# A hybrid trunk step on one core: the side-work unit of a DeltaNet inverse step set from 1.368 to 1.207

## The chip, the core and the metric

The kernel runs on one core of one Trainium2 chip. The metric is the device time of one execution in microseconds (us). The rows shown here come from one profiled execution, which the hardware profiler recorded. In them PE is the matrix engine, PEld its weight load, DVE the vector engine, ACT the scalar engine, POOL the general engine, and SP the engine whose queue starts nearly all transfers (SPq).

## What is computed

Two layers of a trunk run on 640 tokens (128 of a prompt, 512 of a sample), with 1024 channels. Each layer has one wide input projection whose columns feed three branches, a mix, and a feed-forward network. Only the first part of a layer matters here:

```
h  = RMSNorm(x) * (1 + scale1) + shift1
ya = (cb * conv(cc * cx)) @ w_pa              # short gated conv, 4 blocks of 128 channels
yb = attention(q, k, v) @ w_pb                # 8 heads, 2 kv heads, 128 cached + 512 sample keys
yc = (norm(deltanet_fwd + deltanet_bwd) * silu(z)) @ w_pc      # 4 heads, 2 directions
mix = (sigmoid(g0)*ya + sigmoid(g1)*yb + sigmoid(g2)*yc) @ w_o
```

DeltaNet needs, for each head, direction and chunk of 128 tokens, the inverse of a unit triangular matrix. The kernel inverts its 32x32 diagonal blocks by elimination, and joins them with small matmuls to 64x64 and 128x128.

## The kernel before

**Layout.** Channels lie on the 128 partitions and tokens along the free axis, in two halves of 320. Float32 products are made of three matmuls in the fp32r type: each operand is split into a high and a low part (`split`, a cast on ACT at L94 and a subtraction on DVE at L95), and `mm3` (L363 to L365) adds high*high, high*low and low*high. `linear` makes one block of 128 output channels: for eight input blocks, two halves and three products that is 48 matmuls; with four input blocks, as for `w_pc`, it is 24. Its weights come in pieces of 256 KB (`wraw`, issued at L359, three buffers), and the split parts have three buffers each (`whi`, `wlo`).

**Main work and side work.** The first part of each layer is traced from two Python generators. `mainc` holds the chains that wait much: two pairs of DeltaNet heads (`delta_pair`, then `dn_out`), then the keys and values, then eight attention heads (`attn_head`, with the next head's `attn_q` traced inside each). `fillc` holds side work for PE: the z blocks, the conv branch (12 blocks), then for eight output blocks a gate (`g0`) and a `w_pa` product, eight gates `g2` and four gates `g1` (each stored to DRAM in `sgd`), and, once all four heads of DeltaNet are done, the eight `w_pc` products of `branch(l, 2, ...)`. Here they are called pc0 to pc7. Each pc block loads a gate (`sgl`, L536) and the running mix (`mixo`, L542) from DRAM, multiplies (L442), adds (L545) and stores the mix (L547).

`run` decides how the two are interleaved. Each `yield` of the main work names a number of units, and side work is traced until it has caught up:

```
for c in main:
    tm += c * rate
    while fill is not None and tf < tm:
        t = next(fill)          # traces one more piece of side work
        if t is None:
            tf = tm
            break
        tf += t
```

A block of side work counts 6.5 units, a `w_pc` or `w_pa` product 3.2. The units of the main work stand in a list of constants: Y_QKV 1.127, Y_NAT 4.215, Y_EL 1.368, Y_INV 1.962, Y_SCAN 2.959, Y_O 2.917, Y_DO 2.558 for DeltaNet, Y_AK 0.438, Y_AKK 2.07, Y_AQ 1.037, Y_AT 0.446 for attention. The units set an order of tracing and nothing else; no instruction carries one. The order in which the instructions of one engine then run follows the traced order closely, but is not bound to it: an instruction that is ready may be put ahead of an earlier one that is not.

**The inverse.** In `delta_pair`, after the decay terms of two heads, the 20 blocks are gathered in `D32` and transposed on DVE into `Tt` (L985). The elimination takes 30 steps (L987 to L993) of a multiply (L990) and an add (L992) on DVE, each followed by `yield Y_EL`. Four transposes on DVE (L1000) give `RA` and `RB`, each followed by `yield Y_EL` too, so a pair has 34 such yields. The joining follows for four cases of head and direction, each with two `yield Y_INV`: the first matmuls are at L1020, fed by the masks that DVE writes at L1011. Then come five scan steps and the outputs.

**Buffers.** Full-width float32 tiles come from three shared sets. The set F has 16 buffers (NF_), and all of these hold one: the gates and mixes of side work (`sg`, `sgl`, `mixo`), the split DeltaNet outputs `rsh0..3` and `rsl0..3` that all eight pc blocks read (from `resplit(yf, "F")`), and the attention outputs `o0..o7`. An attention output is held from its first write until `resplit(o, "C")`, which is traced after `run` has ended. A head's first write of it is two stages behind its scores (NPD = 2). The set E has three buffers, for `D32`, `Tt`, `RA`, `RB`, the modulation weights `wm` and the 512 KB table `rope` (L617).

Of the kernel before, what the change touches and what calls it, by code (L numbers as in the profile page):

```python
# [43 lines left out]
NSQ = (0, 0, 0, 0, 0, 0, 0, 1)  # L44
ENDG = (3, 7)

Y_QKV, Y_NAT, Y_EL, Y_INV, Y_SCAN, Y_O = 1.127, 4.215, 1.368, 1.962, 2.959, 2.917
Y_AT, Y_AQ, Y_AK, Y_AKK, Y_DO = 0.446, 1.037, 0.438, 2.07, 2.558
PB, PF = 8.0, 11.5

# [1362 lines left out]
```

## Time and profile before

| | us |
|---|---|
| median of 3 runs | 2832.45 |
| lowest, highest | 2823.55, 2837.19 |
| the profiled execution | 2826.17 |
| its span, first to last instruction | 2824.4 |

The mean granted clock of PE in the profiled execution was 0.983 of full speed. The profiled execution is 1.77 us longer than its span. The first parts of the two layers lie at about 59 to 779 us and 1480 to 2179 us of the span. A row of the windows view gives, for a stretch, each engine's busy time with the number of its instructions, then the granted clock and the share and rate of the transfers. Starts in rows are us from the start of the span.

### The profile page before, as it was taken

The numbers are of one execution on the slowest core, as the hardware profiler recorded it, in microseconds if no ns is written. First come the engines' busy times: TensorE is split into PE (matmuls) and PEld (weight loads), VectorE is DVE, ScalarE is ACT, GpSimd is POOL, SyncE is SP. The second block draws the span as 40 slices with busy tenths as digits, with TensorE's granted clock in tenths as the row PEclk, the third lists the DMA queues.
The fourth block names the chain that finished last, engine by engine and source line by source line (L and its number), as shares of the span: only waits on it lengthen the run. The fifth ranks groups of instructions, "written<-read, shape, count | busy, mean of one in ns | idle before, by whom it ended". The sixth has DMA issues, their size and how long they took to land.

```text
span 2824.4 us, 49743 instructions
## 1 busy us (share of the span) xinstructions
PE 2732.8 (97%) x19706; PEld 2599.2 (92%) x19706; DVE 1560.5 (55%) x3297; ACT 1260.3 (45%) x2863; POOL 113.6 (4%) x235
## 2 busy tenths in 40 slices
PE   7999999999999999999989999999998999999998
PEld 3899998999799899999979999989998999999997
DVE  4586564477743744324466865745777456442344
ACT  4533553455534533223455345535555354332343
POOL 1000000000001200000020000000000020000002
PEclk9999999999999999999999999999999999999999
DMA  8552355444264444444442323433331333222231
GB/s 243 70 79 58 79 87 111 81 91 113 89 157 139 146 131 143 130 157 143 134 115 64 76 56 86 91 92 77 101 98 62 95 105 96 76 73 75 77 119 65
DMA packets 390970, 288.17 MB, mean 102 GB/s; under 512 B 19051, under 2 KB 354641, under 8 KB 390737
## 3 DMA queue, kind: packets, MB, share of 16 engines
q1 hardware_dynamic: 390736, 285.00, 39.2%
q8 instruction: 154, 2.52, 0.4%
q14 instruction: 80, 0.65, 0.1%
HBM read 251.86 MB, written 33.07 MB: 101 GB/s over the span
## 4 chain that ended last, share of the span: by engine, by line
PE 82%; DMA 6%; DVE 6%; ACT 4%; issue 1%; SPq 0%; POOL 0%; ACTq 0%; DVEq 0%; POOLq 0%
PE l L363 22%; PE l L364 22%; PE l L365 22%; DMA wraw<-in_w_in_dram 2%; PE pm L324 1%; DMA rowb<-gd 1%; PE ptT L772 1%; ACT p L727 1%; DMA xo<-xd 1%; PE po L782 1%; DMA sgl<-sgd 1%; PE po L784 1%; PE scan L1073 1%; PE kk L948 1%; PE po L783 1%
## 5 line engine op out<-in xcount | busy, mean ns | idle before, releaser
L94 ACT CAST whi<-wraw 128x512 fp32r<-128x512 f32 (+1 forms) x540 | 332.2, 615 | 847.8 <-PE l L364 784.4
L95 DVE TENSOR_TENSOR wlo<-wraw,whi 128x512 fp32r<-128x512 f32 (+1 forms) x540 | 369.0, 684 | 560.8 <-ACT whi L94 532.1
L363 PE MATMUL l<-hh,whi 128*128 128x320 f32 x1856 | 588.3, 317 | 11.5 <-ACT padc L863 6.0
L364 PE MATMUL l<-hl,whi 128*128 128x320 f32 x1856 | 584.4, 315 | 0.0
L365 PE MATMUL l<-hh,wlo 128*128 128x320 f32 x1856 | 583.9, 315 | 0.0
L363 PE MATMUL l<-h2h,whi 128*128 128x320 f32 x1248 | 387.4, 310 | 0.0
L364 PE MATMUL l<-h2l,whi 128*128 128x320 f32 x1248 | 385.3, 309 | 0.0
L365 PE MATMUL l<-h2h,wlo 128*128 128x320 f32 x1248 | 385.3, 309 | 0.0
L363 PEld LDWEIGHTS l<-hh,whi 128*128 128x128 f32 x1856 | 352.2, 190 | 15.7 <-ACT padc L863 6.7
L364 PEld LDWEIGHTS l<-hl,whi 128*128 128x128 f32 x1856 | 353.1, 190 | 1.9
L365 PEld LDWEIGHTS l<-hh,wlo 128*128 128x128 f32 x1856 | 352.9, 190 | 1.5
L363 PEld LDWEIGHTS l<-h2h,whi 128*128 128x128 f32 x1248 | 234.6, 188 | 7.0 <-ACT fs L427 3.1
L364 PEld LDWEIGHTS l<-h2l,whi 128*128 128x128 f32 x1248 | 234.6, 188 | 0.0
L365 PEld LDWEIGHTS l<-h2h,wlo 128*128 128x128 f32 x1248 | 234.6, 188 | 0.0
L363 PE MATMUL l<-ah,whi 128*128 128x320 f32 x544 | 168.9, 310 | 0.0
L364 PE MATMUL l<-al,whi 128*128 128x320 f32 x544 | 168.1, 309 | 0.0
L365 PE MATMUL l<-ah,wlo 128*128 128x320 f32 x544 | 168.0, 309 | 0.0
L152 POOL TENSOR_TENSOR acc<-acc,sqt 128x320 f32<-128x320 f32 x88 | 87.1, 989 | 2000.4 <-ACT sqt L148 1998.7
L363 PE MATMUL l<-rsh,whi 128*128 128x320 f32 x384 | 120.0, 315 | 0.0
L364 PE MATMUL l<-rsl,whi 128*128 128x320 f32 x384 | 118.2, 311 | 0.0
L365 PE MATMUL l<-rsh,wlo 128*128 128x320 f32 x384 | 118.2, 309 | 0.0
L363 PEld LDWEIGHTS l<-ah,whi 128*128 128x128 f32 x544 | 102.2, 188 | 2.2 <-ACT pt L447 1.7
(428 smaller groups left out, 5453.3 us busy)
## 6 DMA issues: line engine op xcount, KB each, us to landing
wraw<-in_w_in_dram SPq DMA_DIRECT2D x256, 256.0 KB, 4.3
wm<-in_w_mod_dram SPq DMA_DIRECT2D x80, 512.0 KB, 4.8
wraw<-in_w_gate_dram SPq DMA_DIRECT2D x88, 256.0 KB, 2.9
wraw<-in_w_up_dram SPq DMA_DIRECT2D x88, 256.0 KB, 3.1
wraw<-in_w_down_dram SPq DMA_DIRECT2D x80, 256.0 KB, 2.8
mixo<-mixd SPq DMA_DIRECT2D x32, 320.0 KB, 5.4
wm<-in_w_mod_dram SPq DMA_DIRECT2D x32, 256.0 KB, 4.4
wraw<-in_w_pb_dram SPq DMA_DIRECT2D x32, 256.0 KB, 4.4
```

Of the source, the lines that this page charges most:

```text
L94: A.copy(hi, src)
L95: V.tensor_sub(lo, src, hi.bitcast(F32))
L152: (V if n == 2 else G).tensor_add(accs[0], accs[0], t)
L324: T.matmul(pm[32 * u:32 * u + 2, 0:256], lhsT=sc[:, k, :], rhs=w[:, u * 256:(u + 1) * 256], start=(n == 0), stop=(n == KD - 1))
L363: T.matmul(out, lhsT=wh, rhs=ah, start=first, stop=False)
L364: T.matmul(out, lhsT=wh, rhs=al, start=False, stop=False)
L365: T.matmul(out, lhsT=wl, rhs=ah, start=False, stop=last)
L727: A.activation(p[:, o_:o_ + w], x, AF.Exp, scale=rc, bias=nb[:, 0:1], accum_out=s[:, i:i + 1])
L772: T.transpose(pt[:, i, q * P:(q + 1) * P], sm_[q][:, kt * P:(kt + 1) * P], ident)
L782: T.matmul(po, lhsT=vh, rhs=th, start=(kt == 0), stop=False)
L783: T.matmul(po, lhsT=vl, rhs=th, start=False, stop=False)
L784: T.matmul(po, lhsT=vh, rhs=tl, start=False, stop=(kt == 4))
```

## The change

One constant changes:

```diff
-Y_QKV, Y_NAT, Y_EL, Y_INV, Y_SCAN, Y_O = 1.127, 4.215, 1.368, 1.962, 2.959, 2.917
+Y_QKV, Y_NAT, Y_EL, Y_INV, Y_SCAN, Y_O = 1.127, 4.215, 1.207, 1.962, 2.959, 2.917
```

Thirty steps of 1.368 are 41.04 units, and 34 steps of 1.207 are 41.04 units: the unit goes down as the number of yields beside it had gone up, from 30 to 34. Before the change the 34 yields count 46.51 units. No instruction is added or removed; side work is traced later against the main work.

## Rows read from the trace of the kernel before

**Rows 1.** The page, part 1: busy time of each engine.

```profile
PE 2732.8 (97%) x19706; PEld 2599.2 (92%) x19706; DVE 1560.5 (55%) x3297; ACT 1260.3 (45%) x2863; POOL 113.6 (4%) x235
```

**Rows 2.** Windows of 20 us: two in the first pair's elimination, layer 0.

```profile
160.00:180.00 20.00, 20.00 (x139) 20.00 (x138) 19.51 (x47) 5.56 (x12) 1.66 (x10) 1.00 0.40 87
180.00:200.00 20.00, 20.00 (x139) 20.00 (x138) 19.31 (x48) 4.60 (x8) 0.00 (x0) 1.00 0.38 67
```

**Rows 3.** Windows after the second pair's elimination, both layers.

```profile
440.00:450.00 10.00, 10.00 (x70) 10.00 (x69) 1.38 (x2) 3.40 (x6) 0.00 (x0) 1.00 1.02 124
450.00:470.00 20.00, 16.69 (x168) 14.41 (x167) 6.50 (x14) 6.00 (x13) 0.00 (x0) 0.74 0.41 109
1840.00:1855.00 15.00, 15.00 (x110) 14.77 (x110) 3.32 (x6) 6.69 (x12) 0.00 (x0) 1.00 0.74 148
1855.00:1870.00 15.00, 13.16 (x123) 11.36 (x123) 5.17 (x11) 4.61 (x10) 0.00 (x0) 0.67 0.34 95
```

**Rows 4.** Windows: attention with side work and its last 40 us, both layers.

```profile
690.00:740.00 50.00, 49.96 (x369) 47.03 (x369) 38.06 (x103) 30.30 (x88) 0.00 (x0) 1.00 0.32 95
740.00:780.00 40.00, 34.48 (x232) 27.70 (x232) 28.61 (x78) 24.32 (x71) 0.00 (x0) 0.91 0.24 79
2090.00:2140.00 50.00, 49.80 (x362) 47.91 (x361) 38.38 (x104) 29.43 (x84) 0.00 (x0) 1.00 0.27 81
2140.00:2180.00 40.00, 31.75 (x197) 27.66 (x195) 27.76 (x77) 24.05 (x71) 0.00 (x0) 0.87 0.04 9
```

**Rows 5.** Who PE waited for, 1480 to 2190 us: total, times, longest.

```profile
PE psc L363 <- ACT p L727: 5.1, 2, 4.1
```

**Rows 6.** DVE: the last w_pc block's addition in each layer (L545).

```profile
715.60 0.83 DVE L545 TENSOR_TENSOR sgl<-sgl,mixo 128x640 f32<-128x640 f32 x1
...
2119.11 0.82 DVE L545 TENSOR_TENSOR sgl<-sgl,mixo 128x640 f32<-128x640 f32 x1
```

**Rows 7.** Chain of waits and SP's queue, layer 0, second pair: start, length.

```profile
434.98 6.73 DMA wraw<-in_w_in_dram
...
443.18 11.17 DMA wraw<-in_w_in_dram
...
436.14 0.34 SPq L617 DMA_DIRECT2D rope<-in_rope_dram  x1
```

**Rows 8.** DVE in order of time, layer 0: end of the first pair's elimination.

```profile
169.87 2.06 DVE L985 STREAM_TRANSPOSE Tt<-D 128x1024 f32<-128x1024 f32 x1
...
204.37 0.09 DVE L994 MEMSET Tt<- 128x32 f32 x1
204.42 0.22 DVE L992 TENSOR_TENSOR Tt<-Tt,tmpE 128x58 f32<-128x58 f32 x1
...
209.87 0.50 DVE L1011 TENSOR_TENSOR Xq<-RB,cst 128x320 f32<-128x320 f32 x1
```

**Rows 9.** PE at L1020: first joining matmuls (min/median/max ns, first and last start).

```profile
L1020 PE MATMUL pw<-RB,nt x21: 191/191/212, 214.4 to 232.0; 32*32 32x32 f32 x21
L1020 PE MATMUL pw<-RB,nt x20: 191/191/212, 1619.4 to 1621.0; 32*32 32x32 f32 x20
```

**Rows 10.** DVE: masks that release the joining, layer 1's first pair.

```profile
1615.99 0.46 DVE L1011 TENSOR_TENSOR Xq<-RB,cst 128x320 f32<-128x320 f32 x1
```

**Rows 11.** Tiles o and mixo: splitting an attention output, loading the mix.

```profile
L94 ACT CAST rsh<-o x16: 723/728/734, 776.6 to 2183.2; 128x640 fp32r<-128x640 f32 x16
L95 DVE TENSOR_TENSOR rsl<-o,rsh x16: 814/818/826, 777.5 to 2184.3; 128x640 fp32r<-128x640 f32 x16
...
DMA to landing us min/median/max: 3.5/5.4/7.2
```

**Rows 12.** Window of 10 us inside layer 0's last 40 us of attention.

```profile
750.00:760.00 10.00, 9.24 (x46) 7.75 (x46) 6.18 (x20) 5.03 (x16) 0.00 (x0) 0.66 0.32 124
```

## The prediction

> **What bounds the kernel now.** I read the page's busy times first. PE is busy for 97% of the span [rows 1], so only time in which PE stands still, or runs at less than full clock, can be won, and time is lost only where PE is newly made to wait. Then I read windows through the first part of a layer, since the constant orders nothing else. In the elimination PE does 139 matmuls in each 20 us and DVE is busy for 19.3 to 19.5 of them [rows 2]: both are full. 20 us / 139 is 0.144 us for a matmul, so a side block of 48 matmuls is 6.9 us of PE and a pc block of 24 is 3.45 us. These two prices carry most of what follows.
>
> PE is not full in two places. One is after the second pair's elimination: in 450 to 470 us of layer 0 it stands still for 20 - 16.69 = 3.3 us, and the granted clock of the stretch is 0.74; in layer 1 it is 15 - 13.16 = 1.8 us at 0.67 [rows 3]. The reader should see a gap and then the lower of the clock's two levels (1.2 in place of 2.4 GHz) behind it. The other is the end of attention, 740 to 780 us and 2140 to 2180 us: 5.5 us and 8.25 us still, clock 0.91 and 0.87 [rows 4]. There the waits are those of softmax (in layer 1 the prompt's scores wait once for 4.1 us for the exponentials on ACT [rows 5]), and no side work is at hand: the last pc block is added at 715.6 us and at 2119.1 us [rows 6], long before attention ends.
>
> **What the change does to the order.** It follows from the yields by addition. A pair's 34 yields go from 46.51 to 41.04 units. The main work of a layer is, before, 123.4 units for the first pair, 126.8 for the second (three `linear` yields more) and 43.4 for keys, values and heads: 293.6. The side work is 16 blocks at 6.5 (z and conv), eight times 9.7, 12 gates at 6.5 and eight pc at 3.2: 285.2. So before, the side work runs out 8.4 units early: pc7 is traced at unit 282.3, in the first stages of head 5. After, the main work is 282.6 units, and pc7 is traced at 282.2, behind head 7's last scores; pc5 comes in head 6's first stage and pc6 in its second. Ahead of the first joining matmul there stood 84.5 units of side work in the first pair and 214.1 in the second; now it is 78.0 and 201.1. That is one block fewer, and then two fewer. Nothing else moves: no instruction is added, and the transfers of a side block go with it on SP's queue, past those of the main work (two weight pieces, a gate store; for pc one weight piece, `sgl`, `mixo` and a store).
>
> **Part 1, the end of attention.** With side work at hand PE does 369 matmuls in 50 us in layer 0, and 362 in layer 1 [rows 4]. At that rate the 232 and 197 of the last 40 us need 31.4 and 27.2 us, so 8.6 and 12.8 us are lost there, waits and low clock together. The three pc blocks that arrive hold 3 x 3.45 = 10.35 us of PE for each layer, which no longer stands elsewhere. From above the gain is 8.6 + 10.35 = 19.0 us (each layer the smaller of what is lost and what arrives). From below it is nothing: softmax's chain of DVE, ACT and PE might be lengthened by as much as is filled. I take pc5 and pc6 as filling, and pc7, traced behind the last scores, as not: 2 x 3.45 = 6.9 us for each layer, 13.8 us in all, because the heads just before, with this same ratio of side work, leave PE still for 0.04 and 0.2 us in 50 [rows 4].
>
> How much is to be had depends on the row that one trusts. The Trainium skill (Perfetto Trace Analysis, Identifying the Most-Contended Engine) says that matmul occupancy judges TensorE badly, since pipelined matmuls blur it, and that LDWEIGHTS occupancy judges it better. By matmul busy time the two ends lose 5.5 + 8.25 = 13.8 us; by weight loads, 27.70 at 47.03 in 50 and 27.66 at 47.91 in 50, they lose 10.6 + 11.1 = 21.7 us [rows 4]. Two thirds of the one would be 9.2 us and a time of 2820.7, of the other 14.4 us and 2815.4; the counts of matmuls agree with the second.
>
> **Part 2, the second pair's joining.** Its stall starts as a transfer. When `Tt` is done with, a buffer of E is free and the 512 KB `rope` load starts, at 436.1 us, between two weight pieces that take 6.7 and 11.2 us to land [rows 7]. PE works off what it has until 450 us (70 matmuls in 10 us, DVE nearly idle [rows 3]), then starves, and the joining is queued behind the starved block. The two stalls cost 3.3 + 1.8 us still and 0.26 x 20 + 0.33 x 15 = 10.2 us of clock, 15.3 us in all. Two blocks fewer ahead of the joining mean that its matmuls can run while those pieces are on their way. But `rope` still starts there, and the joining itself alternates between PE, ACT and DVE and leaves gaps that want side work. Bounds are a gain of 15.3 us (no starving) and a loss as large (it starves twice). I take half of the standstill, 2.6 us, and leave the clock as it is: the transfer that causes the stall is not changed.
>
> **Part 3, the eliminations.** PE now has one block less to do while DVE eliminates. Layer 0's first pair: DVE goes from the first transpose at 169.9 us to the last mask at 210.4 [rows 8], 40.5 us, and PE's first joining matmul starts at 214.4 [rows 9], 4.0 us after. In layer 1 it is 1616.45 and 1619.4, 3.0 us [rows 10, 9]. Taking 6.9 us from in front of it would leave PE 2.9 and 3.9 us early, a loss of up to 6.8 us for both layers, if PE had nothing to put in. From the other side DVE loses a block's work too, and the queues are not bound to the traced order: the memset that follows step 30 ran in front of step 29's add [rows 8]. So I take 0; what hides it is the block traced just behind. In the second pair DVE is done long before PE (1.38 us busy in 440 to 450 us [rows 3]), so two blocks fewer cost nothing.
>
> **Sum.** -13.8 - 2.6 + 0 = -16.4 us. Against the profiled execution that is 2826.2 - 16.4 = 2809.8. This execution is 6.3 us under the median of the runs, 2832.45, so on the median I say 2816.
>
> **The rivals.** *It is only shifted* (2832): the side work is the same in sum, so what fills the last heads is missing earlier, and the standstill comes out in keys and values or heads 0 to 4. For it: pc0's place moves from before head 0's scores to head 2. Against it: in 690 to 740 and 2090 to 2140 us PE is full at this same ratio [rows 4].
>
> *All of it is won* (2798): 19.0 us at the ends and 15.3 us at the joinings, because the joining runs while the pieces land. For it speaks the DVE idle at 440 us [rows 3]; against it the `rope` load [rows 7].
>
> *The F buffers run out* (2848, slower). F has 16. While pc blocks are due, eight are the split DeltaNet outputs, and a pc block needs two (`sgl`, `mixo`). Before, pc7 came with five attention outputs written, 8 + 2 + 5 = 15. After, pc6 comes with six, 16, and pc7 with seven, 17. It must then wait for an attention output to be split, and head 7's own first write needs a buffer as well; behind it on ACT wait its copy and the casts for the next matmuls. Price for each layer: 0.73 + 0.82 us of split, 5.4 us for the mix to land [rows 11] and 0.83 us of add [rows 6], 7.8 us, and behind such a gap 0.34 x 10 = 3.4 us of clock as at 750 us [rows 12]. Twice 11.2 is 22.4 us; pc5 alone still fills, 6.9 us, so +15.5. It decides once a seventh output is written before pc7's mix has its buffer. Against it: pc7's matmuls need no F buffer, only their eviction does, and splitting a finished head early frees one. The Trainium skill (Perfetto Trace Analysis, Optimization Strategy) reads repeated gaps on the engine that should be full as a possible sign that no SBUF or PSUM is left for the next tile; by that the end of attention would keep its gaps, and this rival's 2848 would be the time.
>
> **How the numbers follow.** The forecast (2816) gets 0.44, only shifted 0.28, all won 0.16, F buffers 0.12. The range holds all but the extremes: below it reaches the all-won case at 2798; above, no change with part 3's bound, 2832 + 7 = 2839, and somewhat into the slower case: 2842. A measurement of this kernel can tell about 0.5%, 14 us, from no change. The forecast lies 16 us down, 2 beyond that line, so some 0.6 of its chance counts as faster and the rest as the same: faster 0.16 + 0.27 = 0.43, with a little of the shifted case 0.46; slower 0.12, the F case; the same 0.42.
>
> **What would show it.** Right: pc additions (L545) well after 715.6 us, up to the end of attention; over 250 matmuls in each of the last 40 us of attention, at a clock near 1; first joining matmuls of the second pairs some 14 us earlier. Part 1 is wrong if the last heads are as empty as before, with L545 after the splits of the attention outputs; part 2 if the stall beside `rope` is longer; part 3 if PE waits at L1020 in the first pairs. A changed feed-forward part would mean that the order after attention matters, which I left out.

## The result and the profile after

The changed kernel takes 2785.7 us (median of 4 runs, 2784.52 to 2792.69), the kernel before beside it 2828.0 us: a ratio of 0.9855, interval 0.9816 to 0.9895. The forecast was 2816, its range 2798 to 2842. The direction is right, the time lies 12 us below the range. The forecast stood on 2832.45 us for the kernel before, the median of three runs; beside the change that median is 2828.0, and 4.5 of the 30 us between forecast and time come of that alone.

The profiled execution took 2784.52 us, 41.65 less than the one of before. All that PE does is as before (19706 matmuls); the page's first part answers to [rows 1]:

```profile
PE 2710.3 (97%) x19706; PEld 2584.0 (93%) x19706; DVE 1554.9 (56%) x3297; ACT 1257.7 (45%) x2863; POOL 113.1 (4%) x235
```

PE's share is again 97%, and the page alone would hide the change. What has to be counted is PE's lost time place by place: idle time (length less PE busy) and clock loss ((1 - granted clock) times length). I added both up over windows of 5 us of the two first parts, leaving out windows that lose under 0.3 us; "2.4 + 1.8" is idle + clock loss in us:

| place | before, layer 0 | layer 1 | after, layer 0 | layer 1 | won |
|---|---|---|---|---|---|
| first pair's joining (205; 1590 us) | 0 | 0 | 1.3 | 2.2 | -3.5 |
| decay-row loads `rowb` (350; 1755 us) | 2.4 + 1.8 | 2.4 | 0 | 0 | 6.6 |
| second pair's joining (450; 1855 us) | 3.3 + 5.2 | 1.8 + 5.0 | 0 | 0 | 15.3 |
| first loads of stored gates `sgl` (615; 2015 us) | 2.4 + 1.7 | 3.2 + 1.7 | 0 | 0 | 9.0 |
| end of attention (750; 2150 us) | 5.1 + 3.4 | 7.8 + 5.1 | 2.8 | 2.8 | 15.8 |

The sum is 43.2 us, 41.65 was measured; with every window of the whole span it is 40.5 us, so little changed outside the two first parts. The table is of one execution of each kernel, and the clock loss in it differs from execution to execution (last section). Of 52.3 us lost before, 23.9 were clock loss: after a gap the rows show the lower of the two clock levels, and in this kernel that cost nearly as much as the gaps themselves. After the change these places hold 9.1 us of gaps, and in this execution none of them is followed by the lower clock.

Windows of the kernel after: the end of attention in both layers, which answers to [rows 4].

```profile
690.00:720.00 30.00, 29.95 (x226) 28.29 (x225) 23.15 (x59) 16.26 (x46) 0.00 (x0) 1.00 0.44 137
720.00:760.00 40.00, 36.85 (x286) 31.67 (x284) 29.67 (x81) 24.42 (x68) 0.00 (x0) 1.00 0.54 165
...
2070.00:2100.00 30.00, 29.94 (x217) 28.72 (x216) 24.71 (x66) 18.14 (x52) 0.00 (x0) 1.00 0.29 96
2100.00:2137.00 37.00, 34.23 (x245) 31.36 (x244) 28.37 (x78) 22.54 (x66) 0.00 (x0) 1.00 0.27 88
```

The last 40 us hold 286 matmuls, where there were 232, at full clock. The last attention output is copied at 758.0 us (778.3 before), and in layer 1 at 2136.4 (2178.8).

Windows of the kernel after: first joining, decay rows, second joining (which answers to [rows 3]), gate loads, and layer 1's first joining.

```profile
205.00:210.00 5.00, 3.72 (x33) 3.39 (x31) 4.93 (x10) 1.65 (x4) 0.42 (x1) 1.00 0.09 15
340.00:360.00 20.00, 20.00 (x139) 20.00 (x138) 13.52 (x23) 11.23 (x24) 0.00 (x0) 1.00 0.54 112
425.00:445.00 20.00, 19.86 (x192) 18.18 (x191) 8.56 (x17) 8.23 (x16) 0.00 (x0) 1.00 0.94 148
590.00:615.00 25.00, 24.86 (x185) 24.38 (x184) 18.23 (x49) 16.54 (x45) 0.00 (x0) 1.00 0.29 84
1590.00:1595.00 5.00, 2.81 (x21) 2.55 (x19) 4.90 (x11) 1.38 (x3) 0.00 (x0) 1.00 0.21 52
```

Two of these places could be seen in the trace of before, and the prediction passed them over. Windows of the kernel before: decay rows and gate loads, layer 0, then layer 1.

```profile
340.00:360.00 20.00, 17.61 (x110) 17.35 (x109) 13.02 (x24) 6.79 (x15) 1.69 (x13) 0.91 0.36 95
600.00:620.00 20.00, 17.60 (x120) 17.01 (x120) 15.54 (x44) 9.85 (x28) 0.00 (x0) 0.94 0.61 139
...
1740.00:1760.00 20.00, 17.56 (x127) 17.30 (x127) 12.33 (x32) 8.64 (x24) 1.69 (x13) 1.00 0.38 96
2000.00:2020.00 20.00, 16.84 (x124) 16.25 (x123) 14.77 (x41) 10.86 (x31) 0.00 (x0) 1.00 0.42 117
```

In each, PE stands still for 2.4 to 3.2 us; a walk through the whole first part in equal windows finds them.

What was newly lost is in PE's waits (who waits <- for whom: total, times, longest), layer 0 and layer 1 of the kernel after:

```profile
PE pw L1020 <- DVE RB L1000: 1.3, 1, 1.3
...
PE pw L1020 <- DVE RB L1000: 2.2, 1, 2.2
```

### The profile page after: what moved, and what is told of

Same layout as the page of the kernel before. It is cut to its first block, busy times and chain, and to the rows that moved or that the text cites. A ratio compares the mean times of both kernels' runs of the same rounds, so it can differ in the third digit from the quotient of the medians.

```text
span 2782.6 us, 49763 instructions
## 1 busy us (share of the span) xinstructions
PE 2710.3 (97%) x19706; PEld 2584.0 (93%) x19706; DVE 1554.9 (56%) x3297; ACT 1257.7 (45%) x2863; POOL 113.1 (4%) x235
## 4 chain that ended last, share of the span: by engine, by line
PE 84%; DVE 6%; DMA 5%; ACT 3%; issue 1%; SPq 0%; POOL 0%; ACTq 0%; DVEq 0%; POOLq 0%
PE l L363 23%; PE l L364 23%; PE l L365 23%; DMA wraw<-in_w_in_dram 2%; PE pm L324 1%; DMA wm<-in_w_mod_dram 1%; PE ptT L772 1%; PE po L782 1%; PE scan L1073 1%; PE po L784 1%; PE sco L363 1%; PE po L783 1%; DVE wlo L95 1%; PE kk L948 1%; PE scan L1081 1%
```

## The experiments

Each is compared with the kernel before, run beside it on the same chip. The medians of before lie between 2820.8 and 2823.6 in these comparisons, so ratios are to be compared, not times. Lost PE time is given as idle + clock loss, as in the table.

**1. `att_only`: the new order from attention on, the old one in DeltaNet.** The unit stays 1.368; both pairs' 10.94 units are taken back in one step before keys and values.

```diff
+            yield -10.94
             yield from attn_kv(l, kv)
```

> Y_EL stays 1.368; 10.94 units are taken from the main work's count just ahead of keys and values, so that DeltaNet's order is that of before and attention's that of after. Theory of places (each of four stalls goes by its own shift): the lost time at the ends of attention (8.5 and 12.9 us before) falls to about 3 us in each layer and the stall at the first gate loads (4.1 and 4.9 us) goes, 25 us in all, so about 2801 for a profiled execution of 2826; the stalls after the second pair's elimination (9.3 and 6.8 us) and at 350 and 1755 us stay. Rival, that the gain comes from DeltaNet's order alone: under 5 us.

Measured: 0.991 (0.9885 to 0.9936), 2798.78 us. Windows of it, layer 0: decay rows, second joining, gate loads, end of attention.

```profile
345.00:360.00 15.00, 12.59 (x76) 12.33 (x75) 8.80 (x16) 5.37 (x12) 0.22 (x7) 0.89 0.47 114
450.00:470.00 20.00, 16.82 (x178) 14.42 (x178) 6.98 (x16) 6.00 (x13) 0.00 (x0) 0.74 0.37 101
600.00:625.00 25.00, 24.87 (x184) 24.09 (x183) 19.68 (x54) 18.09 (x51) 0.00 (x0) 1.00 0.25 72
740.00:760.00 20.00, 17.60 (x148) 13.14 (x146) 14.90 (x43) 10.44 (x31) 0.00 (x0) 1.00 0.72 238
```

In layer 0 the first two stalls stay as they were, the gate loads' goes, and the end of attention falls to 2.4 us without clock loss (2.6 us in layer 1). In layer 1 the decay rows' stall stays, and at the second joining the gap stays (1.6 us, before 1.8) but the lower clock does not follow it, which the expectation had not foreseen. The medians differ by 22 us. So the order in attention wins some 22 us by itself, and that includes the gate loads, not only the ends.

**2. `dn_only`: the new order in DeltaNet, the old one from attention on.**

```diff
-..., Y_EL, ... = ..., 1.368, ...
+..., Y_EL, ... = ..., 1.207, ...
...
+            yield 10.94
             yield from attn_kv(l, kv)
```

> Y_EL is 1.207; 10.94 units are added just ahead of keys and values, so that DeltaNet's order is that of after and attention's that of before. Theory of places: the stalls after the second pair's elimination (15.4 us with the clock) and at the loads of the broadcast decay rows (6.5 us) go, the first pairs' new waits at L1020 (3.5 us) come, so 18 us less than before, about 2808; the ends of attention stay as before. Rival, that everything is won at the ends of attention: no change, 2826.

Measured: 0.9981 (0.9967 to 0.9996), 2815.27 us. Windows of it: second joining in layer 0, gate loads in layer 1, end of attention in layer 0.

```profile
425.00:445.00 20.00, 19.33 (x190) 17.66 (x189) 7.94 (x17) 8.33 (x16) 0.00 (x0) 1.00 0.91 144
1995.00:2010.00 15.00, 11.87 (x70) 11.29 (x69) 7.23 (x19) 4.91 (x14) 0.00 (x0) 0.77 0.49 137
735.00:765.00 30.00, 24.01 (x165) 18.11 (x163) 21.95 (x65) 17.18 (x54) 0.00 (x0) 0.94 0.25 88
```

The picture is the mirror of the first: the decay rows are full, the second joinings lose 0.7 us and nothing, the waits at the first joinings are there (1.3 and 2.2 us, the second with 3.4 us of clock loss), gate loads and ends stay. The places answer as expected; the time does not. The profiled execution is 14.1 us below that of before, the medians on this chip differ by 5.6 only. The two profiles are single draws: that of before (2826.17) lies 5.3 us above the median of before here, that of `dn_only` 3.2 us below its own. By the intervals of the ratios `att_only` wins 18 to 32 us, `dn_only` 1 to 9, and the whole change 36 to 47 (`after_again`, below). That allows the halves to add up to the whole, but does not show it.

**3. `pair2`: the new unit in the second pair alone.** One block fewer, not two, then stands ahead of the second joining.

```diff
-..., Y_EL, ... = ..., 1.368, ...
+..., Y_EL, ... = ..., (1.368, 1.207), ...
...
-            yield Y_EL
+            yield Y_EL[hp]
```

> The unit is 1.368 in the first pair and 1.207 in the second. Theory of places: the first pair's joining waits no longer for DVE (3.5 us of after are not paid); the decay rows' stall (6.5 us) stays, since the second pair begins with side work where it was; the second pair's joining has one block fewer ahead of it, and its stall should be about halved (8 us of 15); attention is shifted by 5.5 units, half the way, for half of 25 us. Together some 20 us less than before, 2806. If two blocks are needed at the joining, 13 us less.

Measured: 0.9973 (0.9953 to 0.9993), 2814.2 us. Windows of it: second joining in both layers.

```profile
445.00:465.00 20.00, 16.77 (x173) 14.32 (x173) 5.81 (x13) 5.04 (x11) 0.00 (x0) 0.74 0.58 89
1845.00:1865.00 20.00, 18.54 (x160) 16.00 (x160) 5.87 (x12) 5.58 (x13) 0.00 (x0) 0.66 0.51 101
```

The stall is not halved, it is all there: 8.3 us in each layer, against 8.5 and 6.8 before. The decay rows stay too (3.8 and 3.7 us), the gate loads are gone, the ends still lose about 9 and 8 us. The expectation missed. (The profiled execution, 2822.44 us, is the slowest of ten; the fastest took 2803.64.)

**4. `pair2_1046`: two blocks fewer, all of it in the second pair.** As the one before, with (1.368, 1.046).

> The unit is 1.368 in the first pair and 1.046 in the second: 10.95 units are taken away in the second pair alone, so two blocks fewer stand ahead of the second joining, as after the change, and the first pair is that of before. Theory of places: the stall after the second elimination (15 us) goes, the end of attention and the first gate loads go as in the run that moved attention alone (25 us), the stall at 350 and 1755 us (6.5 us) stays, and the first pairs pay no wait at L1020: about 40 us less than before, near the time of after. Rival, that the joining stall depends on the first pair's order too: it stays, 25 us less.

Measured: 0.9878 (0.9846 to 0.9911), 2788.28 us. Windows of it, layer 0: decay rows and second joining.

```profile
345.00:360.00 15.00, 12.70 (x77) 12.44 (x76) 8.90 (x16) 5.40 (x13) 0.09 (x3) 0.89 0.44 115
435.00:455.00 20.00, 20.00 (x246) 17.15 (x245) 8.09 (x19) 8.57 (x18) 0.00 (x0) 1.00 0.80 142
```

With two blocks fewer the second joining's stall is gone in both layers, also when both are taken from the second pair; the decay rows, which lie ahead of the second pair's yields, stay (4.0 and 3.5 us). At the first joining of layer 1, where the order is that of before, PE loses 0.9 + 3.5 us here, which the expectation did not have. So PE's gap at the second joining of layer 0 is 3.3, 3.2 and 0 us for none, one and two blocks fewer: a step, not a slope. In the other executions with two blocks fewer it is 0.1 to 0.8 us; the clock loss behind it is less regular (experiment 10).

**5. `norope`: the kernel before without the `rope` load.** The table is filled with a constant, so the rotary embedding computes with other numbers.

```diff
-        SY.dma_start(out=rt, in_=I["rope"])
+        G.memset(rt, 0.5)
```

> The kernel before without the load of the rope table: its tile is filled with a constant on POOL, so the rotary part computes with other numbers. If the rope transfer starves the second pair's joining by taking the transfers' time (part 2 of the prediction), the stall of 9.3 and 6.8 us goes and the time falls by about 15 us. If the stall comes from the number of side blocks queued ahead of the joining and from the order of SP's queue, it stays and the time falls by less than 4 us.

Measured: 0.997 (0.9953 to 0.9987), 2816.11 us.

**6. `sgd_pool`: the kernel before, the stores of gates issued from POOL's queue in place of SP's.**

```diff
-            SY.dma_start(out=sgd[b, m], in_=gate(l, b, m))
+            G.dma_start(out=sgd[b, m], in_=gate(l, b, m))
```

> The kernel before with only the stores of the gates (sgd, 320 KB each) issued from POOL's queue in place of SP's; the tracing order is that of before. Without the rope load a weight piece still took 10.9 us to land while the transfers went at some 55 GB/s. If weight pieces are slow there because they stand behind a gate store that SP's queue has issued, they land in about 4 us, PE does not starve after the second elimination, and 12 to 15 us are won, though two more side blocks still stand ahead of the joining. If the pieces are slow because the stores take the same transfer engines, or the number of blocks ahead decides by itself, the stall stays and the time changes by less than 4 us.

Measured: 0.9957 (0.9941 to 0.9973), 2811.92 us.

**7. `norope_sgd`: both of these** (the rotary embedding again with a constant).

> The kernel before with both: the gate stores from POOL's queue, and no load of the rope table (its tile is filled with a constant, so the rotary part computes with other numbers). Each alone took the joining stall away in layer 1 and left 1.4 to 1.8 us of standstill with 5.1 to 5.2 us of clock in layer 0. If the stall is a pile-up of transfers on weight pieces, it is now gone in both layers, 15 us less than before and under 1 us of standstill after the second elimination of layer 0. If two blocks ahead of the joining decide by themselves, layer 0's stall stays at 6 us or more.

Measured: 0.9957 (0.9935 to 0.998), 2811.89 us. Windows at the second joining, layer 0 and layer 1, of `norope`, `sgd_pool` and `norope_sgd` in turn; for the last also the 5 us ahead of it.

```profile
450.00:465.00 15.00, 13.58 (x126) 11.76 (x125) 5.28 (x12) 4.60 (x10) 0.00 (x0) 0.66 0.32 97
1840.00:1855.00 15.00, 14.05 (x126) 13.32 (x124) 2.77 (x4) 7.47 (x14) 0.00 (x0) 1.00 0.66 120
```

```profile
450.00:465.00 15.00, 13.21 (x124) 11.12 (x122) 5.17 (x11) 4.60 (x10) 0.54 (x1) 0.66 0.32 94
1840.00:1855.00 15.00, 15.00 (x163) 14.01 (x161) 3.04 (x7) 7.35 (x14) 1.08 (x2) 1.00 0.62 133
```

```profile
440.00:445.00 5.00, 5.00 (x36) 5.00 (x35) 0.30 (x2) 1.11 (x3) 0.00 (x0) 1.00 1.01 52
445.00:455.00 10.00, 8.34 (x86) 7.57 (x85) 2.17 (x4) 5.72 (x11) 0.56 (x2) 1.00 0.69 154
```

In layer 1 taking away either transfer is enough: 0.9 us is left without `rope`, none with the stores moved. In layer 0 neither is: 1.4 + 5.2 and 1.8 + 5.1 us. With both gone 1.7 us remain there, and the clock stays up. So none of the three expectations came out as written: the stall neither goes nor stays. In layer 0 the gap is about half of before's 3.3 us in all three, and taking both away leaves no less than taking one; only the clock loss differs. `rope` is then not *the* cause; it is one of several transfers that meet. Even without it a weight piece took 10.94 us to land (440.06 us, in `norope`), and in 440 to 445 us of `norope_sgd` the transfers are busy for all of the time at 52 GB/s. What slows them is not settled.

**8. `pool_queue`: the kernel before, decay rows (L907) and stores of the mix (L547) issued from POOL's queue.** It asks whether the other two places are SP's queue standing behind one entry.

```diff
-                SY.dma_start(out=mixd[m], in_=sg)
+                G.dma_start(out=mixd[m], in_=sg)
...
-        SY.dma_start(out=t, in_=gd[l][:, dh, :].partition_broadcast(P))
+        G.dma_start(out=t, in_=gd[l][:, dh, :].partition_broadcast(P))
```

> The kernel before, with the loads of the decay rows (L907) and the stores of the mix (L547) issued from POOL's queue instead of SP's; the order of tracing is that of before. If the stalls at 350 and 1755 us and at 610 and 2015 us come from a load or store that waits on SP's queue and holds weight pieces behind it, they go: 6.5 and 9.0 us, about 15 us less than before, while joinings and ends of attention stay as they are. If they come from the transfers themselves or from DVE being late, they stay and the time changes by less than 4 us.

Measured: 1.0005 (0.999 to 1.0019), 2824.17 us. Windows of it, layer 0: decay rows, and the gate loads.

```profile
350.00:360.00 10.00, 9.45 (x65) 9.18 (x64) 5.03 (x8) 6.74 (x13) 0.00 (x0) 1.00 0.46 123
610.00:620.00 10.00, 7.73 (x56) 7.17 (x55) 5.14 (x14) 5.17 (x15) 0.54 (x1) 1.00 0.52 157
```

SP's longest waits in 560 to 620 us, first of the kernel before, then of this one:

```profile
SPq L359 <- DVE wlo L95: 25.3, 11, 4.0
SPq L547 <- DVE sgl L545: 10.4, 2, 9.4
```

```profile
SPq L359 <- DVE wlo L95: 48.3, 11, 13.5
```

The decay-row stall falls from 2.4 + 1.8 to 0.6 us (in layer 1 from 2.4 to 0.4); in layer 0 a wait of 2.1 us at 375 us takes its place. But it is not weight pieces that PE waits for there. Waits in 335 to 362 us: PE's and ACT's of the kernel before, then ACT's of this one, then of the kernel after:

```profile
PE l L363 <- ACT padc L863: 2.4, 1, 2.4
ACT egl L962 <- DMA rowb<-gd: 8.0, 2, 6.5
```

```profile
ACT egl L962 <- DMA rowb<-gd: 7.0, 2, 4.8
```

```profile
ACT egl L962 <- DMA rowb<-gd: 6.8, 2, 3.8
```

PE waits for a bank that ACT is to copy out (`padc`, L863), and that copy stands in ACT's order behind an operation (`egl`, L962) that waits for the second decay row: SP issues it at 345.80 us, once DVE has read the last of the buffer (L957), and it takes 7.9 us to land. What holds PE there is the copy behind the load, on ACT. In `pool_queue` two of these copies run ahead of the wait, at 345.65 us, and it is shorter.

At the gate loads the mix store's 9.4 us wait goes, and the next entry of the same queue waits 13.5 us instead, for the subtraction `wlo` that stands behind softmax in DVE's order. The stall stays (2.3 us idle), so the store was not its cause, and there the expectation missed. PE waits there for the multiplication L442, and in 600 to 622 us of the kernel before DVE waits for the gate:

```profile
DVE sgl L442 <- DMA sgl<-sgd: 3.2, 1, 3.2
```

The load is issued at 606.51 us and takes 9.8 us to land; in `pool_queue` it is issued at 603.60 and takes 9.6. In the kernel after DVE waits for no gate there. In this run the second joinings lose 10.4 and 9.5 us, more than before, so the time shows no gain from the decay rows.

**9. `moved_end`: the first pair keeps 1.368 up to its joining and gives its 5.47 units back behind it; the second pair has 1.207.** If the wait at the first joining is the price of the change, this version should not pay it. On top of the edit of `pair2`:

```diff
+        if hp == 0:
+            yield -5.47
         vns, sts = {}, {}
```

> The first pair keeps 1.368 and gives 5.47 units back behind its joining; the second pair has 1.207. From there on the order is that of after. Theory of places: all that after gains, without the waits at L1020 that it pays in the first pairs (1.3 and 2.2 us): 3 us less than after, some 45 us less than before. Rival, that the first pair's shorter elimination is itself a part of the gain: slower than after.

Measured: 0.9848 (0.9825 to 0.9871), 2780.99 us, 41 us less than before. Beside the changed kernel it stands in the next two runs.

**10 and 11. `moved_end_again` and `after_again`: that version and the changed kernel on one chip.**

> The kernel with 1.368 in the first pair, 5.47 units given back behind its joining and 1.207 in the second pair, beside the changed kernel on one chip: 3 to 5 us faster than it, by the waits at L1020 that it does not pay.

> The changed kernel itself, for the comparison on one chip: 1.4 to 1.5 per cent faster than before.

Measured: 0.9838 (0.9818 to 0.9858), 2781.04 us, and 0.9853 (0.9835 to 0.9872), 2783.47 us. Windows at the first joining of layer 0: `moved_end_again`, with its second joining, then `after_again`.

```profile
205.00:215.00 10.00, 10.00 (x80) 9.57 (x79) 7.71 (x13) 2.66 (x6) 0.42 (x1) 1.00 0.31 57
430.00:450.00 20.00, 19.17 (x149) 16.77 (x148) 5.57 (x12) 5.52 (x13) 0.00 (x0) 0.66 0.63 74
```

```profile
205.00:215.00 10.00, 8.78 (x93) 7.45 (x91) 5.95 (x12) 1.94 (x5) 0.42 (x1) 0.78 0.29 40
```

The wait at the first joining does go. But `moved_end_again` loses 0.8 + 6.8 us at the second joining of layer 0, where two blocks fewer stand ahead of it as in the kernel after, which loses nothing there. So two blocks fewer take most of the gap away, not always the clock loss. In time the two differ by 2.4 us and their intervals overlap: this is not told apart from no difference, and the 3 to 5 us that were expected are not shown.

**12. `el_1046`: one step further, 1.046 in both pairs.**

> The unit goes on down to 1.046 in both pairs, 10.95 units for each. Theory of places: no stall is left to win but about 3 us at each end of attention; the first pairs' elimination lacks a second block, 6.9 us more of waiting at L1020 in each layer, 10 to 14 us in all, and three pc blocks are left over behind attention: 5 to 15 us slower than after. Rival, that later side work is always better here: faster than after.

Measured: 1.006 (1.0034 to 1.0087), 2838.52 us: slower than before and, by the ratios, some 2% above the changed kernel; 5 to 15 us were expected. Windows of it in layer 0: both joinings, end of attention; then two of PE's waits, and two pieces of the chain of waits at the end of attention (start, length).

```profile
205.00:225.00 20.00, 17.67 (x182) 14.90 (x181) 9.77 (x20) 3.39 (x9) 0.42 (x1) 0.66 0.16 28
425.00:445.00 20.00, 17.52 (x134) 16.05 (x133) 10.43 (x25) 5.12 (x10) 0.00 (x0) 0.74 0.44 109
760.00:775.00 15.00, 9.22 (x66) 6.88 (x65) 10.04 (x16) 6.60 (x13) 0.00 (x0) 0.77 0.78 252
```

```profile
PE l L363 <- DVE sgl L442: 4.9, 1, 4.9
PE pw L1020 <- DVE RB L1000: 4.8, 2, 2.5
```

```profile
761.44 0.84 DVE rsl L95
762.29 4.85 DMA mixo<-mixd
```

Now both joinings wait for the elimination, each gap is followed by the lower clock (6.8 us of clock loss at the first joining), and the end of attention loses as much as before in layer 0: 5.8 + 3.4 us. There the prediction's rival *the F buffers run out* is seen: the load of the mix starts when the first attention outputs have been split, takes 4.85 us to land, and PE waits 4.9 us for the multiplication L442 of a pc block behind it. The decay rows stall again, too (2.0 + 1.7 us in layer 0). Both the expectation and its rival missed. The good stretch of this constant is narrow.

## Why the prediction was wrong, by its steps

**"PE is not full in two places"** is the step that failed outright. There were four that the change reaches. The decay rows (6.6 us) and the first gate loads (9.0 us) together are 15.6 us that the sum did not hold, and both lie in windows that [rows 2 to 4] leave out. Experiments 1 and 2 show which half of the change removes each: the order in DeltaNet the first, the order in attention the second. At the decay rows the trace shows PE waiting for a copy on ACT that stands behind the load of a decay row, at the gate loads for the load of a gate, 9.8 us in landing (experiment 8). Why the gate lands in time in the new order stays open: SP's wait for `wlo` is as long in the kernel after (13.8 us in 560 to 620 us), without a stall.

**"I take half of the standstill, 2.6 us, and leave the clock as it is"** (part 2) is the term that was mis-sized: 15.3 us were won, idle and clock both, which is the upper bound that the same part names. The argument for the small value, "the transfer that causes the stall is not changed", was wrong twice. Experiments 5 to 7 show that `rope` is not the sole cause. And the transfers need not be faster for the stall to go: in the kernel after they are busy for 0.94 of 425 to 445 us, and in that stretch PE does 192 matmuls, many of them the joining's small ones, because the joining now starts at 433.2 us, 7.3 behind `rope`, and not at 450.7, 14.6 behind it. Nor is the joining "queued behind the starved block" on PE. The wait of PE, then ACT in order of time, in the kernel before (in brackets how long ACT stood still first, and what ended that):

```profile
PE pw L1020 <- ACT Wp L1022: 3.3, 1, 3.3
451.98 0.62 ACT L94 CAST whi<-wraw 128x512 fp32r<-128x512 f32 x1 [2.20 <-DMA wraw<-in_w_in_dram]
...
454.45 0.62 ACT L94 CAST whi<-wraw 128x512 fp32r<-128x512 f32 x1 [1.52 <-DMA wraw<-in_w_in_dram]
...
455.43 0.28 ACT L1022 COPY Wp<-pw 32x160 f32<-32x160 f32 x1
```

The same in the kernel after:

```profile
433.73 0.62 ACT L94 CAST whi<-wraw 128x512 fp32r<-128x512 f32 x1 [1.75 <-PE pw L1020]
...
434.71 0.28 ACT L1022 COPY Wp<-pw 32x160 f32<-32x160 f32 x1
```

The first joining matmuls run at 450.7 us; PE's next ones wait for ACT's copy `Wp`, and that copy stands on ACT behind two casts of weight pieces that land late. After the change ACT waits for no weight piece there, and the copy comes 1.5 us behind the first joining matmul. In `moved_end_again` ACT does wait 2.45 us for a piece, and PE 0.8 us for the copy. In these traces, then, the gap goes by whether the pieces ahead of the copy have landed when the joining starts.

The size holds some luck. 10.2 of the 15.3 us are clock loss, and that does not go by the order alone: in `att_only` the gap at layer 1's second joining brought none, in `moved_end_again` one of 0.8 us brought 6.8 us.

**Part 1** (the end of attention, 13.8 us) was right in mechanism and size: 15.8 us. By its own test, pc7 is added at 739.67 us and the first split of an attention output runs at 756.26. That is 2 us more than two blocks were to fill, so pc7, counted as not filling, may have filled a part. The weight-load count gave 21.7 us lost; idle plus clock loss on the fine windows gives 21.4, while matmul busy time alone gave 13.8; 8.5 of the 21.4 us are clock loss, in which PE looks busy. The Trainium skill (Perfetto Trace Analysis, Identifying the Most-Contended Engine) judges TensorE by LDWEIGHTS busy time and by its share of the peak FLOPs, not by matmul busy time, because matmuls are pipelined. This trace agrees: 21.7 us by weight loads beside 21.4.

**Part 3** (the eliminations, 0) cost 3.5 us, inside its bound of 6.8. The block traced behind hid the 2.9 and 3.9 us only in part; PE waits at L1020, by which the prediction itself called this part wrong. The first joining starts at 208.5 us (214.4 before), and with the first pair's unit put back (`moved_end_again`) the wait is gone. That the cost stayed inside the bound is luck: in `after_again`, the same kernel, the two gaps were followed by 6.9 us of clock loss, 10.2 us in all, and the bound has no clock in it.

**The rivals.** *It is only shifted* did not happen: no place in the heads before the last lost what the end won (29.95 of 30 us busy from 690 us). *The F buffers run out* did not happen either: pc7's addition at 739.67 us comes 16.6 us before any attention output is split. One step further it does (`el_1046`). The Trainium skill (Perfetto Trace Analysis, Optimization Strategy) takes repeated gaps as a possible sign of missing buffers. No buffer was added here and the gaps at the ends fell from 12.9 to 5.6 us, so in the kernel before they were missing work. *All of it is won* (2798) came nearest, and its joining half came true in full; it is still 12 us too slow, because it too knows only two places.

## What to carry to other kernels

Before pricing a change of order, walk through all of the span that it reorders in equal windows and add up idle time and clock loss of the bounding engine for each place; a page at 97% hid 52 us. Where PE waits for a copy on another engine, look at what stands ahead of that copy in the engine's order: at the second joining and at the decay rows it was an operation that waited for a load. The gap at the second joining went in a step and not in proportion, so half of it was no safe middle. And this constant, which only sets an order, has a narrow good stretch: 1.207 gave 0.9855 and 1.046 gave 1.006 of the time with 1.368.

## What the runs showed of the hardware

A gap of 1.4 us is followed by 5.2 us of clock loss at one place (`norope`, layer 0), a gap of 2.2 us in the kernel after by none; in another execution of the same kernel that wait was followed by 3.4 us (`after_again`, clock 0.78 in 205 to 215 us in layer 0, 0.82 in 1590 to 1600). A gap of 0.8 us was followed by 6.8 us (`moved_end_again`), one of 1.6 us by none (`att_only`, layer 1). Gaps of the same length do not cost the same from run to run, and the times move with the clock: the fastest execution of `pair2` has a span of 2801.9 us at a mean granted clock of 0.990, the slowest 2820.5 us at 0.984. (1 - clock) times span is 28.0 and 45.1 us, which is 17.1 of the 18.6 us between them.

Transfers that are busy for the whole of a stretch moved 52 to 54 GB/s there (440 to 445 us of `norope`, `sgd_pool` and `norope_sgd`) and 171 GB/s in the same stretch of the kernel before; at a share of 0.72 they moved 238 GB/s elsewhere (`att_only`, 740 to 760 us). A share near 1 does not say that much is moved.
